# Up projections of a gated MLP by Strassen's seven products, with the down projection dealt between them, in a two-layer encoder kernel on Trainium2

## The chip, the cores and the metric

One core of one Trainium2 chip. The metric is the device time of one execution in microseconds, median of several runs. The kernel before takes 1583.78 us (three runs, 1583.47 to 1584.88).

## The reference, cut to what matters

Two layers of an encoder on 512 tokens of width 1024, all in float32. The attention part of each layer is left out here, since the change does not touch it. The rest of a layer is a gated MLP of width 2816:

```python
hf = rms_norm(x, ffn_norm_g[l])
u = depthwise_conv(hf @ ffn_w_up[l], ffn_conv_w[l], ffn_conv_b[l])   # 512x1024 @ 1024x5632
u_gate, u_val = u[..., :D_FF], u[..., D_FF:]
x = x + (jax.nn.silu(u_gate) * u_val) @ ffn_w_down[l]                # 512x2816 @ 2816x1024
```

## The kernel before

Every matrix product is made of three: each float32 operand is held as a high half, rounded to the type that TensorE multiplies fast (`fp32r`), and a low half, the rest. `mm3` (it calls `mm`, L376) issues high x high, high x low and low x high; low x low is left out. TensorE's moving operand is 512 tokens wide, its stationary operand a 128x128 block of weights or activations.

Weights come as float32 from HBM, in transfers of 128x1024 (`raw<-w`, on SP's queue). `w_split` makes the halves of a piece of 128x512: ScalarE copies it to the high half (`wh<-raw`, L224), and GpSimd, or VectorE where a rule in `pick` says so, subtracts (`wl<-raw,wh`, L231). `wnext` hands TensorE the next piece and has the pieces up to `LA = 3` places ahead split. Lines of the helpers stand for all engines: L224 is every ScalarE activation, L231 every `tensor_tensor`, L235 every `scalar_tensor_tensor`.

The order in which each engine's instructions stand is fixed when the program is built. A class `Clock` counts time by a table of costs per instruction, runs the chains of follow-up work (`chain`, `at`, `need`, `done`) when their inputs should be ready, and so decides where in each engine's queue an instruction stands. At run time each engine works through its queue strictly in that order.

The MLP of a layer works on features x tokens. 22 chunks of 128 features have a gate part and a value part; I call the two a chunk pair. For each part `feat_major` issues 8 x 3 matmuls of 512 columns into one PSUM bank (banks `acc`, `ST` and `AV` in turn), with the weights stationary and the normalised input's halves `HH`, `HL` moving. The normalisation by token (`rbc`) comes after the product. `up_evac` then chains, per part: a VectorE multiplication by `rbc` out of PSUM (`u<-ps_..,rbc`), ScalarE's middle tap of the convolution (`a<-u,prm`), and the two outer taps on VectorE (`a<-u,prm,a`). For the gate follows ScalarE's SiLU; for the value follow the product of the two (`a<-a,a`, VectorE), and its halves (`ah<-a` on ScalarE, `al<-a,ah` on GpSimd). When all 22 chunks are there, the down projection runs: 8 output blocks, each a sum over 22 x 3 matmuls of 512 columns, and a VectorE addition into the residual `XM`. The last output block of the last layer is done in two halves of 256 tokens (`half`), with one bank each (`mi`, `S`).

Of the kernel before, what the change touches and what calls it, by code (L numbers as in the profile page):

```python
# [18 lines left out]
P = 128  # L19
# [13 lines left out]
RAW = 3  # L33
EXTRA = (("q", 2, (2, 5)), ("n", 2, (6, 7)), ("v", 1, (1, 3)))
# [7 lines left out]
LA = 3  # L42
# [7 lines left out]
D_SUM = 2.0  # L50
REST = 0.4
# [33 lines left out]
def _widths():  # L85

    r = [384] * KC + [T] * 8 + [T] * KC + [288] * MID + [T] + [288] * (KC - MID)
    for br in (2, 1, 0):
        late = []
        for k, _ in _order(br):  # L90
            if k in "nv":
                late = WIDTHS[k]
            else:
                r += WIDTHS[k][:1] + late + WIDTHS[k][1:]
                late = []
    return r + [T] * (2 * KC) + [T] * (4 * FC) + [T] * (2 * FC)


def _stream():

    pieces, slots = [], []
    for wd in _widths() * L:
        if len(slots) <= KC or slots[-1] + wd > 1024:
            slots.append(0)
        pieces.append((len(slots) - 1, slots[-1], wd))
        slots[-1] += wd
    return pieces, slots
# [155 lines left out]
def trunk(ctx: ExitStack, tc: tile.TileContext, x, w, prm, gb, cst, out):  # L263
# [57 lines left out]
    pieces, swidth = _stream()  # L321
    soff = np.concatenate([[0], np.cumsum(swidth)]) * P
    st = {"dma": 0, "split": 0, "use": 0}
    raws, halves = {}, {}

    def w_dma():
        i = st["dma"]
        t = slot("raw") if i < KC else rawp.tile([P, 1024], F32, tag="raw", name=f"raw{i}")
        SY.dma_start(t[:, :swidth[i]], w[int(soff[i]):int(soff[i + 1])].rearrange("(p c) -> p c", p=P))
        raws[i] = t  # L330
        st["dma"] += 1

    def w_split():
        j = st["split"]
        sl, off, wd = pieces[j]
        r = raws[sl][:, off:off + wd]
        hi = hlp.tile([P, T], F32R, tag="wh", name=f"wh{j}")
        lo = hlp.tile([P, T], F32R, tag="wl", name=f"wl{j}")
        ck.fin = ck.now
        if j == 0:  # L340
            V.tensor_copy(hi[:, :wd], r)
        else:
            A.activation(hi[:, :wd], r, AF.Copy)
        e = V if j < KC + 3 else pick(W_BIAS, ck.fin + ck.SEM)
        ck.free[e.kind] = max(ck.free.get(e.kind, 0.0), ck.fin + ck.SEM)
        e.tensor_tensor(lo[:, :wd], r, f(hi[:, :wd]), ALU.subtract)
        done("w", j)
        halves[j] = (hi, lo)
        st["split"] += 1
        if j + 1 == len(pieces) or pieces[j + 1][0] > sl:  # L350
            at(ck.fin - ck.now, lambda: w_until(sl + RAW))

# [6 lines left out]
    def w_until(i):  # L359
        while st["dma"] <= min(i, len(swidth) - 1):  # L360
            w_dma()

    def w_ahead(j):
        while st["split"] <= min(j, len(pieces) - 1):
            w_until(pieces[st["split"]][0])
            w_split()

    def wnext():
        j = st["use"]
        w_ahead(j + LA if j > LA else j)  # L370
# [4 lines left out]
    def mm(o, lhsT, rhs, start, stop):  # L375
        PE.matmul(o, lhsT=lhsT, rhs=rhs, start=start, stop=stop)  # L376
        ck.to(ck.now + max(0.107, rhs.shape[-1] / 2370.0))
# [5 lines left out]
    def mm3(o, lh, ll, rh, rl, start, stop):  # L383
        mm(o, lh, rh, start, False)
        mm(o, lh, rl, False, False)
        mm(o, ll, rh, False, stop)
# [14 lines left out]
    MQ, MK = [[cp.tile([P, 4, 4, 96], F32, tag=f"{n}{g}", name=f"{n}{g}") for g in range(2)] for n in ("MQ", "MK")]  # L401
# [132 lines left out]
    def layer(l, sq, xsrc):  # L534
# [6 lines left out]

        gt = slot("gb")
# [913 lines left out]
        def up_evac(c, part, acc, tag):  # L1456
            ci = c + part * FC
            u, a = slot("u"), slot("a")

            def scale():  # L1460
                V.tensor_tensor(u[:, :T], acc, fin["rbc"][:, :T], ALU.mult)
                free(tag)

            steps = [
                ([("rbc", G2)], scale),
# [6 lines left out]
            if part == 0:  # L1472
# [4 lines left out]
                steps.append(gate)  # L1477
            else:
                ah, al = slot("ah", F32R), slot("al", F32R)
                act[c] = (ah, al)  # L1480

                def prod():
                    V.tensor_tensor(a[:, :T], a[:, :T], gated.pop(c)[:, :T], ALU.mult)
                steps += [([("gate", l, c)], prod), *split(ah[:, :T], al[:, :T], a[:, :T], eng=G),
                          lambda: done("act", l, c)]
            chain(*steps)

        n = 0
        norm_begin(G2, sq)
        for c in range(FC):  # L1490
            for part in range(2):
                tag = tags[n % 3]
                n += 1
                acc = ps(tag)
                for i, _ in enumerate(feat_major(acc, G2)):
                    norm_finish(G2, fin, n == 3 and i == 6)
                up_evac(c, part, acc, tag)

        last = l == L - 1
        sq = None if last else slot("sq")  # L1500
        idx, tail = 0, []
        two = [ps(t) for t in ("mi", "S")] if last else None

        def half(n, kc, wh, wl):
            ts = slice(256 * n, 256 * n + 256)
            mm3(two[n][:, :256], wh, wl, act[kc][0][:, ts], act[kc][1][:, ts], kc == 0, kc == FC - 1)
# [6 lines left out]
        for m in range(KC):  # L1513
            tag = tags[m % 3]
            acc = ps(tag)
            for kc in range(FC):
                if idx % 4 == 0:
                    wh, wl = wnext()
                need(("act", l, kc))
                ws = slice((idx % 4) * P, (idx % 4) * P + P)  # L1520
                idx += 1
                if not (last and m == KC - 1):
# [209 lines left out]
```

## Time and profile before

| | |
|---|---|
| median of the runs | 1583.78 us |
| the profiled execution's own time | 1584.02 us |
| its span, first to last instruction | 1581.9 us |
| up projections, layer 0 and layer 1 | about 438 to 688 us, 1219 to 1458 us |
| down projections | about 688 to 808 us, 1458 to 1579 us |
| busy share of the span: PE, DVE, ACT, POOL | 99%, 60%, 50%, 65% |

PE is TensorE, DVE VectorE, ACT ScalarE, POOL GpSimd, SP the engine that issues most transfers. A group's row reads: line, engine, operation, output<-inputs, sizes, count, then busy microseconds and the mean nanoseconds of one, then idle time of the engine just before these instructions and what ended it. An instruction's record overlaps the next one's on the same engine, on PE by much: the pace is read from one start to the next, not from the durations.

### The profile page before, as it was taken

The numbers are of one execution on the slowest core, as the hardware profiler recorded it, in microseconds if no ns is written. First come the engines' busy times: TensorE is split into PE (matmuls) and PEld (weight loads), VectorE is DVE, ScalarE is ACT, GpSimd is POOL, SyncE is SP. The second block draws the span as 40 slices with busy tenths as digits, with TensorE's granted clock in tenths as the row PEclk, the third lists the DMA queues.
The fourth block names the chain that finished last, engine by engine and source line by source line (L and its number), as shares of the span: only waits on it lengthen the run. The fifth ranks groups of instructions, "written<-read, shape, count | busy, mean of one in ns | idle before, by whom it ended". The sixth has DMA issues, their size and how long they took to land.

```text
span 1581.9 us, 20358 instructions
## 1 busy us (share of the span) xinstructions
PE 1567.1 (99%) x7098; PEld 1308.3 (83%) x7098; DVE 946.0 (60%) x1335; ACT 790.7 (50%) x1440; POOL 1023.1 (65%) x901
## 2 busy tenths in 40 slices
PE   9999989999999999999999999899999999999999
PEld 8888878888888888888898888788888888888888
DVE  6867886875267777711046688878652677777000
ACT  5557766763444444432254577676634444444221
POOL 3974876854667666664578658668546676666542
PEclk9999999999999999999999999999999999999999
DMA  6432234314323222233334322343242233223331
GB/s 202 127 115 73 74 91 143 106 62 141 101 91 107 93 94 96 100 115 109 107 111 130 110 74 74 94 138 103 67 147 94 85 109 100 94 93 107 107 126 47
DMA packets 86070, 164.43 MB, mean 104 GB/s; under 512 B 25040, under 2 KB 47056, under 8 KB 85968
## 3 DMA queue, kind: packets, MB, share of 16 engines
q1 hardware_dynamic: 81072, 162.93, 32.4%
q8 instruction: 56, 0.92, 0.2%
q10 hardware_dynamic: 4896, 0.21, 0.2%
q14 instruction: 46, 0.38, 0.1%
HBM read 149.41 MB, written 13.63 MB: 103 GB/s over the span
## 4 chain that ended last, share of the span: by engine, by line
PE 91%; DVE 4%; ACT 2%; DMA 1%; issue 1%; POOL 0%; SPq 0%; ACTq 0%; DVEq 0%
PE ps_acc L376 40%; PE ps_AV L376 22%; PE ps_ST L376 22%; PE ps_S L376 4%; PE ps_mi L376 3%; DVE XM L231 1%; DVE mgl L231 1%; ACT mgh L224 1%; DMA XM<-x 1%; DVE gt L235 0%; DVE sq L231 0%; DMA raw<-w 0%; ACT wh L224 0%; DVE vt L235 0%; ACT ph L224 0%
## 5 line engine op out<-in xcount | busy, mean ns | idle before, releaser
L231 POOL TENSOR_TENSOR wl<-raw,wh 128x512 fp32r<-128x512 f32 (+3 forms) x494 | 668.3, 1364 | 397.5 <-ACT wh L224 377.3
L224 ACT ACTIVATE wh<-raw 128x512 fp32r<-128x512 f32 (+3 forms) x521 | 308.9, 607 | 137.8 <-PE ps_ST L376 46.0
L235 DVE SCALAR_TENSOR_TENSOR a<-u,prm,a 128x511 f32<-128x511 f32 x176 | 243.9, 1388 | 92.6 <-ACT a L224 86.8
L376 PE MATMUL ps_acc<-HH,wh 128*128 128x512 f32 x592 | 231.7, 391 | 3.3 <-DVE vm L231 2.9
L376 PE MATMUL ps_acc<-HH,wl 128*128 128x512 f32 x592 | 231.2, 391 | 0.0
L376 PE MATMUL ps_acc<-HL,wh 128*128 128x512 f32 x592 | 231.1, 390 | 0.0
L376 PEld LDWEIGHTS ps_acc<-HH,wh 128*128 128x128 f32 x592 | 111.4, 188 | 26.4 <-issue 4.4
L376 PEld LDWEIGHTS ps_acc<-HH,wl 128*128 128x128 f32 x592 | 111.2, 188 | 23.8
L376 PEld LDWEIGHTS ps_acc<-HL,wh 128*128 128x128 f32 x592 | 111.3, 188 | 22.8
L376 PE MATMUL ps_AV<-HH,wh 128*128 128x512 f32 x288 | 112.3, 390 | 0.0
L376 PE MATMUL ps_AV<-HH,wl 128*128 128x512 f32 x288 | 112.2, 390 | 0.0
L376 PE MATMUL ps_AV<-HL,wh 128*128 128x512 f32 x288 | 112.2, 390 | 0.0
L231 POOL TENSOR_TENSOR al<-a,ah 128x512 fp32r<-128x512 f32 x44 | 58.0, 1319 | 83.5 <-ACT ah L224 79.4
L239 DVE TENSOR_REDUCE nm<-ps_S 128x1 fp32r<-128x512 f32 x128 | 87.7, 685 | 36.0 <-PE ps_S L376 34.6
L376 PE MATMUL ps_ST<-HH,wh 128*128 128x512 f32 x240 | 93.6, 390 | 0.0
L376 PE MATMUL ps_ST<-HL,wh 128*128 128x512 f32 x240 | 93.4, 389 | 0.0
L376 PE MATMUL ps_ST<-HH,wl 128*128 128x512 f32 x240 | 93.4, 389 | 0.0
L224 ACT ACTIVATE ah<-a 128x512 fp32r<-128x512 f32 x44 | 27.8, 632 | 128.8 <-DVE a L231 128.8
L224 ACT ACTIVATE a<-u,prm 128x512 f32<-128x512 f32 x88 | 70.9, 808 | 23.4 <-DVE u L231 23.2
L224 ACT ACTIVATE a<-a 128x512 f32<-128x512 f32 x44 | 27.6, 632 | 104.7 <-DVE a L235 104.7
L224 ACT ACTIVATE HH<-XM,prm 128x512 fp32r<-128x512 f32 x32 | 23.1, 722 | 103.5 <-DVE XM L231 53.7
L224 ACT ACTIVATE ps_ST<-ps_ST 128x512 f32<-128x512 f32 x86 | 49.8, 582 | 32.9 <-PE ps_ST L376 31.2
(374 smaller groups left out, 3734.9 us busy)
## 6 DMA issues: line engine op xcount, KB each, us to landing
raw<-w SPq DMA_DIRECT2D x230, 512.0 KB, 3.4
raw<-w SPq DMA_DIRECT2D x14, 384.0 KB, 3.1
XM<-x SPq DMA_DIRECT2D x16, 256.0 KB, 3.7
dtq<-tr SPq DMA_DIRECT2D x16, 192.0 KB, 1.9
dtk<-tr SPq DMA_DIRECT2D x16, 192.0 KB, 1.9
tf<-dtq SPq DMA_DIRECT2D x48, 64.0 KB, 2.0
tf<-dtk SPq DMA_DIRECT2D x48, 64.0 KB, 2.1
xsp<-XM SPq DMA_DIRECT2D x8, 256.0 KB, 2.0
```

What stands on the lines that cost most here:

```text
L224: return self.eng.activation(out, in_, func, **k)
L231: return self.eng.tensor_tensor(out, *a)
L235: return self.eng.scalar_tensor_tensor(out, *a)
L239: return self.eng.tensor_reduce(out, in_, *a, **k)
L376: PE.matmul(o, lhsT=lhsT, rhs=rhs, start=start, stop=stop)
```

## The change

Of the 22 chunk pairs of a layer, 5 (group 0) are computed as before. For the other 17, the 2x2 block matrix of (gate and value part) x (even and odd 128-feature blocks of the input) meets the 2x2 matrix of (even and odd input blocks) x (first and second 256 tokens), and `product` multiplies them with Strassen's seven products (Winograd's form) in place of eight. One product is 4 x 3 matmuls of 256 columns.

- **Token side**, once per layer (`build_forms`): the normalised input is formed explicitly (`hn`, 8 VectorE instructions of 512 columns), GpSimd makes its sums (`tt`, 16 of 256 columns), and the 7 x 4 forms are split into halves (`tf`, 28 ScalarE copies and 28 VectorE subtractions of 256 columns).
- **Weight side**, per pair (`w_form`): four pieces of 128x512 are loaded, each by a transfer of its own. Three of the seven forms are plain pieces; the four others are sums that VectorE makes (`raw<-raw,raw`, `s<-raw,raw` ...), and their low halves are made on VectorE too.
- **Low halves by transfer** (`by_transfer`): for the three plain forms, and for all weights of group 0, ScalarE writes the high half and its negative, and a transfer issued by GpSimd adds the raw weights to the latter. GpSimd's subtraction goes.
- **After the products**, per pair: four ScalarE copies of 256 columns out of PSUM (`sx`), and four VectorE additions of 256 columns (`u<-ps_..,sx`) in place of the two multiplications by `rbc`. The chain from the convolution on is kept.
- **Down projection** in five groups of chunks (`SIZES`): the blocks of one group are dealt between the products of the next (`_ffn`), with bank `mi` or `S`; each group ends in its own addition to the residual, so 40 in place of 8 per layer. The matmuls are as many as before. 8 blocks of group 3 and all of group 4 come after the last pair.
- The weights are made `LAF = 5` places ahead near such products.

```diff
-LA = 3
+LA, LAF = 3, 5
+SIZES = (5, 4, 4, 4, 5)
+KEEP = 2
+FORMS = ("11", "12", "1", "22", "2", "4", "3")
+SPOTS = ("22", "2", "4", "3")
...
+    def by_transfer(hi, lo, r):
+        A.activation(hi, r, AF.Copy)
+        A.activation(lo, f(hi), AF.Copy, scale=-1.0)
+        ck.free["Pool"] = max(ck.free.get("Pool", 0.0), ck.fin + ck.SEM)
+        ck.took("Pool", D_ISSUE)
+        nc.gpsimd.dma_start(f(lo), r, accum_op=ALU.add)
+        ck.fin += D_ADD
...
+        dst, x, y, op, keys, gone = {
+            "1": (a21, a21, a22, ALU.add, [], None),
+            "2": (s2, a21, a11, ALU.subtract, [("sum", pi, "1")], 0),
+            "4": (a12, a12, s2, ALU.subtract, [("sum", pi, "2")], None),
+            "3": (s2, a22, s2, ALU.subtract, [("sum", pi, "4"), ("form", pi, "2")], 3)}[form]
+        def total():
+            V.tensor_tensor(dst, x, y, op)
...
+        def low():
+            V.tensor_tensor(lo[:, :T], dst, f(hi[:, :T]), ALU.subtract)
...
+        chain((keys, total), lambda: A.activation(hi[:, :T], dst, AF.Copy), low, after=0.0)
...
     def wnext():
         j = st["use"]
-        w_ahead(j + LA if j > LA else j)
+        n = LAF if any(units[min(i, len(units) - 1)][0] not in "pu" for i in (j, j + LAF)) else LA
+        w_ahead(j + n if j > LA else j)
...
+        def product(c, name):
...
+            for q in range(4):
+                need(("tf", l, name, q))
+                ws, d = slice(q * P, q * P + P), forms[name, q]
+                mm3(o, wh[:, ws], wl[:, ws], d[:, 0:256], d[:, 256:512], q == 0 and name in ("11", "12", "1", "22"),
+                    q == 3, name not in ("12", "22"))
...
+            if name == "11":
+                aside(sa[:, lo], "s1")
+            elif name == "12":
+                chain(([("s1", l, c)], add(u[:, lo], sa[:, lo], "ST")))
+            elif name == "1":
+                aside(sb[:, lo], "s5")
+            elif name == "22":
+                aside(sb[:, hi], "s4", "ST")
+            elif name == "2":
+                aside(sa[:, hi], "s2")
+            elif name == "4":
+                chain(([("s2", l, c)], add(u[:, hi], sa[:, hi], "AV")), *convolve(c, 0, u))
             else:
+                chain(([("s4", l, c)], add(v[:, hi], sb[:, lo])), add(v[:, lo], sb[:, hi], "acc"), *convolve(c, 1, v))
...
+        for kind, *tok in _ffn():
+            {"u": plain, "f": product, "d": down}[kind](*tok)
```

The order of the instructions outside the two MLP parts is the same in both kernels, on every engine. Three places within them:

TensorE's queue, in the up projection of layer 0, before: one part of a pair, 24 such rows to a bank.

```order
L376 MATMUL ps_acc_5266<-HH,wh_5223 128x512
L376 MATMUL ps_acc_5266<-HL,wh_5223 128x512
L376 MATMUL ps_acc_5266<-HH,wl_5224 128x512
```

The same queue in the changed kernel, at the end of product "22" of a pair of group 2 and the start of the dealt block behind it (`tf` a token form, `fh`, `fl` the halves of a weight form made by transfer).

```order
L507 MATMUL ps_ST_6284<-tf_4735,fh_6173 128x256 x2
L507 MATMUL ps_ST_6284<-tf_4735,fl_6174 128x256
L507 MATMUL ps_ST_6284<-tf_4742,fh_6173 128x256 x2
L507 MATMUL ps_ST_6284<-tf_4742,fl_6174 128x256
L507 MATMUL ps_mi_6310<-HH,wh_6187 128x512
L507 MATMUL ps_mi_6310<-HL,wh_6187 128x512
L507 MATMUL ps_mi_6310<-HH,wl_6188 128x512
```

Up to eight matmuls of 512 columns on one input block pair have become seven times three of 256 columns, and the down projection's blocks stand between the products.

VectorE's queue, layer 0, before: one chunk pair from the gate's multiplication to the product of the two parts.

```order
L231 TENSOR_TENSOR u_5704<-ps_acc_5662,rbc_4676 128x512
L235 SCALAR_TENSOR_TENSOR a_5705<-u_5704,prm_92,a_5705 128x511 x2
L231 TENSOR_TENSOR u_5746<-ps_ST_5706,rbc_4676 128x512
L235 SCALAR_TENSOR_TENSOR a_5747<-u_5746,prm_92,a_5747 128x511 x2
L231 TENSOR_TENSOR a_5747<-a_5747,a_5705 128x512
```

The same queue in the changed kernel, the first twelve rows of one pair's round in group 2 (`raw` and `s` are weights and their sums, `sx` the copies of other products, `XM` the residual). The round ends with the rest of these: a low half, a tap, the addition of the next pair's first half, the product of the parts, a sum and two low halves.

```order
L289 TENSOR_TENSOR raw_6104<-raw_6104,raw_6118 128x512
L289 TENSOR_TENSOR XM<-ps_mi_6310,XM 128x512
L289 TENSOR_TENSOR wl_6349<-raw_6104,wh_6348 128x512
L289 TENSOR_TENSOR u_6216<-ps_AV_6263,sx_6218 128x256
L293 SCALAR_TENSOR_TENSOR a_6366<-u_6216,prm_91,a_6366 128x511 x2
L289 TENSOR_TENSOR u_6217<-ps_acc_6220,sx_6219 128x256 x2
L289 TENSOR_TENSOR s_963_6417<-raw_6104,raw_6039 128x512
L289 TENSOR_TENSOR XM<-ps_S_6372,XM 128x512
L293 SCALAR_TENSOR_TENSOR a_6399<-u_6217,prm_91,a_6399 128x511
L289 TENSOR_TENSOR wl_6416<-s_963_6417,wh_6415 128x512
L289 TENSOR_TENSOR raw_6064<-raw_6064,s_963_6417 128x512
L293 SCALAR_TENSOR_TENSOR a_6399<-u_6217,prm_91,a_6399 128x511
```

The seven instructions of a pair have become 19: eight for weight forms and two for the residual have come in among them, and two multiplications have become four half-width additions.

GpSimd's queue, layer 0, before: some two chunk pairs' worth.

```order
L231 TENSOR_TENSOR wl_5004<-raw_4887,wh_5003 128x512
L231 TENSOR_TENSOR wl_5026<-raw_4931,wh_5025 128x512
L231 TENSOR_TENSOR wl_5048<-raw_4931,wh_5047 128x512
L231 TENSOR_TENSOR wl_5070<-raw_4975,wh_5069 128x512
L231 TENSOR_TENSOR al_5045<-a_5043,ah_5044 128x512
```

The same queue in the changed kernel, one pair of group 2 (here the activation's low half is written to `HL`, whose old content is used up).

```order
L289 TENSOR_TENSOR wl_6382<-raw_6120,wh_6381 128x512
L289 TENSOR_TENSOR wl_6459<-raw_6120,wh_6458 128x512
L289 TENSOR_TENSOR HL<-a_6399,HH 128x512
L420 DMA fl_6500<-raw_6232 128x512
L420 DMA fl_6518<-raw_6258 128x512
L420 DMA fl_6562<-raw_6312 128x512
```

Five subtractions per pair (four for its up weights, one for its activation) have become three (two for the dealt down weights) and three issues of adding transfers.

More of the change, by code (lines that the diff above doesn't have):

```diff
@@ L539, in col @@
             return pr[:, i:i + 1]
+        MQ, MK = [[mp.tile([P, 4, 4, 96], F32, tag="m", name=f"{n}{l}{g}") for g in range(2)] for n in ("MQ", "MK")]
         gt = slot("gb")
@@ L1489, in layer, with prod @@
[L1489 to L1497, printed above, removed]
+                return steps + [gate]
+            ah, al = act[c] = keep_act(c)
+            def prod():
+                V.tensor_tensor(a[:, :T], a[:, :T], gated.pop(c)[:, :T], ALU.mult)
```

375 lines of the change are left out of this document (286 added, 89 removed).

## The prediction

> **What bounds the kernel now.** I read the page first, then the chain of work that ended last, then the two MLP parts by stretches and groups.
>
> ```profile
> span 1581.9 us, 20358 instructions
> ...
> PE 1567.1 (99%) x7098; PEld 1308.3 (83%) x7098; DVE 946.0 (60%) x1335; ACT 790.7 (50%) x1440; POOL 1023.1 (65%) x901
> ...
> PEclk9999999999999999999999999999999999999999
> ```
>
> TensorE is busy 99% of the span at the full granted clock. "Busy" can hide a slow pace, so I look at pieces of the chain in order of time: one part of a pair (24 matmuls of 512 columns) and one output block of the down projection (66).
>
> ```profile
> 1229.63 5.45 PE ps_AV L376 x24
> ...
> 1458.12 14.96 PE ps_acc L376 x66
> ```
>
> 5.44 to 5.45 us for 24 and 14.96 for 66 are both 0.2267 us a matmul. A pair costs 48 x 0.2267 = 10.88 us. And TensorE hardly waits for anyone; the longest rows of its waits, over the whole program:
>
> ```profile
> PE ps_acc L376 <- DVE vm L231: 2.9, 2, 1.5
> PE ps_ST L376 <- ACT vt L224: 2.5, 2, 1.3
> PE ps_AV L376 <- DVE ph L247: 1.7, 2, 0.9
> ```
>
> So the time goes with TensorE's own work, until another engine can't keep up. The other engines during layer 0's up projection:
>
> ```profile
> core 0: us, PE busy (x) PEld busy (x) DVE busy (x) ACT busy (x) POOL busy (x), PEclk, DMA share, GB/s
> 448.50:688.00 239.50, 239.50 (x1058) 198.35 (x1057) 168.05 (x155) 107.84 (x177) 162.28 (x111) 1.00 0.30 99
> ```
>
> DVE and POOL are busy some 70% there already. That is the reserve which the change draws on.
>
> **Term 1: TensorE's work.** The pace of 256 columns is in the trace: the last output block of the last layer is done in two halves, 132 matmuls.
>
> ```profile
> 1562.68 0.28 PE L376 MATMUL ps_mi<-ah,wh 128*128 128x256 f32 x1
> ...
> 1578.39 0.28 PE L376 MATMUL ps_S<-ah,wl 128*128 128x256 f32 x1
> ...
> 1562.68:1578.52 15.84, 15.84 (x133) 15.78 (x131) 1.12 (x2) 0.00 (x0) 0.67 (x1) 1.00 0.05 18
> ```
>
> 131 steps in 15.71 us are 0.120 us each, a little over half of 0.2267, though weight loads (PEld) fill 15.78 of the 15.84 us. A pair by seven products is 7 x 12 = 84 such matmuls, 10.08 us: 0.80 less than 10.88. For 17 pairs in two layers that is 34 x 0.80 = **27.2 us** off. One eighth of the work would be 46; the fixed part of each matmul takes the rest. Group 0 and the down projection's matmuls are as many as before, and the order outside the MLP is the same, so nothing else changes on TensorE unless it waits.
>
> **Term 2: can VectorE keep up?** What it costs per instruction, and what it loses beside GpSimd, from the groups of layer 0's up projection:
>
> ```profile
> L231 POOL TENSOR_TENSOR wl<-raw,wh 128x512 fp32r<-128x512 f32 x89 | 135.2, 1534 | 32.3 <-ACT wh L224 32.1
> L235 DVE SCALAR_TENSOR_TENSOR a<-u,prm,a 128x511 f32<-128x511 f32 x88 | 122.1, 1390 | 46.9 <-ACT a L224 43.5 <-POOL wl L231 1.9
> L224 ACT ACTIVATE wh<-raw 128x512 fp32r<-128x512 f32 x88 | 54.0, 616 | 0.7 <-issue 0.7
> L224 ACT ACTIVATE a<-u,prm 128x512 f32<-128x512 f32 x44 | 35.5, 808 | 11.4 <-DVE u L231 11.3
> L231 POOL TENSOR_TENSOR al<-a,ah 128x512 fp32r<-128x512 f32 x22 | 29.0, 1319 | 41.7 <-ACT ah L224 39.7 <-PE ps_acc L376 2.0
> L231 DVE TENSOR_TENSOR a<-a,a 128x512 f32<-128x512 f32 x22 | 16.2, 737 | 1.3 <-ACT a L224 0.6
> ```
>
> and the shortest, median and longest of them over both layers, with the two halves at the end:
>
> ```profile
> L235 DVE SCALAR_TENSOR_TENSOR a<-u,prm,a x176: 739/1658/1885, 450.1 to 1461.1; 128x511 f32<-128x511 f32 x176
> L231 DVE TENSOR_TENSOR a<-a,a x44: 691/693/1667, 457.6 to 1462.8; 128x512 f32<-128x512 f32 x44
> L231 DVE TENSOR_TENSOR u<-ps_ST,rbc x30: 676/692/692, 448.6 to 1458.2; 128x512 f32<-128x512 f32 x30
> L231 DVE TENSOR_TENSOR XM<-ps_mi,XM x1: 425/425/425, 1577.6 to 1577.6; 128x256 f32<-128x256 f32 x1
> ```
>
> A tap of the convolution takes 0.74 us at its shortest and 1.66 in the median; with one operand in PSUM it is 0.69 and never more. The long ones are those that meet a subtraction on GpSimd:
>
> ```profile
> 570.48 2.98 POOL L231 TENSOR_TENSOR wl<-raw,wh 128x512 fp32r<-128x512 f32 x2
> 570.74 3.27 DVE L235 SCALAR_TENSOR_TENSOR a<-u,prm,a 128x511 f32<-128x511 f32 x2 [0.95 <-ACT a L224]
> ```
>
> Two taps beside two subtractions: 3.27 for 1.48, so 0.9 us lost to each. Over the stretch the taps lose 88 x (1.390 - 0.739) = 57 us to its 111 GpSimd subtractions: **0.52 us per GpSimd subtraction** on average, since not each meets a tap. I call this price p; it is the number on which the result hangs.
>
> A pair of groups 2 and 3 in the changed kernel gives VectorE: 8 weight sums and low halves and one product of 512 columns, taken at 0.69 (same operation and operands as `a<-a,a`), 6.21; 4 taps at 0.74, 2.96; 4 additions of 256 columns out of PSUM at 0.425, 1.70; 2 residuals at 0.69, 1.38. Together 12.25 us. To it come waits within the fixed order. Before, 43.5 us of waiting for ScalarE in 44 parts are 1.0 us a part: a tap stands straight behind the addition that ScalarE must first work on. Now one of the two parts has other work in between, but the low half of form "3" stands straight behind its sum and waits for a copy of 0.62 with two others queued ahead of it: 1.0 again, 2.0 per pair, 14.25 us. GpSimd does 3 subtractions, costing 3p. TensorE needs 10.08 + 8 blocks x 3 x 0.2267 = 15.52 us for the same pair.
>
> By groups, VectorE against TensorE per pair, at p = 0, 0.52 and 1.0:
> - Groups 2 and 3 (8 pairs): 14.25, 15.8, 17.25 against 15.52. Late by 0, 0.3, 1.7.
> - Group 1 (4 pairs, 10 dealt blocks, 3.5 subtractions): 14.25, 16.1, 17.75 against 16.88. Late by 0, minus 0.8, 0.9.
> - Group 4 (5 pairs, 4.8 blocks, 1.2 residuals, 2.2 subtractions): 13.7, 14.8, 15.9 against 13.34. Late by 0.4, 1.5, 2.6. Here the pairs stand closest, and it is where I expect the waits.
> - Group 0, once `rbc` is there, has 43 us. VectorE gets 10 multiplications, 8 `hn`, about 20 taps, 4 products, 28 half-width subtractions and 4 weight steps: 6.9 + 5.9 + 14.8 + 2.8 + 11.9 + 2.8 = 45 us by records; these overlap by some 0.08 each where they stand close (about 74 of them), so 39. GpSimd's 16 half-width sums and 4 subtractions add about 12p: 39, 45.5, 51. Late by 0, 2, 8; group 1 gives the 2 back.
>
> A pair has 9 weight places, so five places ahead are 8.6 us. A form needs 0.69 + 0.62 + 0.69 with hand-overs, 2.2, and some 2.1 behind others in the queue. **4.3 us** of lateness per layer cost nothing. Beyond it TensorE waits in full, for weights. Behind the last pair stand 8 + 4 blocks, 8.2 us, before the last activation is needed, against a chain of some 6.5; there VectorE has no next pair's 5.5 us of forms to make and can catch up.
>
> Lateness per layer at p = 0.52: 8 x 0.3 + 5 x 1.5 = 9.9, minus 4.3, so 5.6 of waiting; **11 us** in two layers. At p = 0 none; at p = 1.0, 8 + 3.6 + 13.6 + 13 = 38, minus 4.3, 67 us in two layers. I take 0.52, the mean of the nearest rows: VectorE's queue will be denser than before, which raises the share of subtractions that meet something, but 6 of its 19 instructions read PSUM, and some of what is lost falls into the 2.0 us in which it waits anyway.
>
> A rule of the Trainium skill speaks against the change: in "SBUF — State Buffer", section "Who interferes with whom", a VectorE instruction with two SBUF inputs and a GpSimd instruction that reads SBUF exclude each other for the whole instruction, whoever comes first. The trace agrees in kind: 0.74 against 1.66, and never over 0.69 with PSUM. By that rule alone every subtraction that meets VectorE's queue could cost up to its whole 1.29 us; the measured 0.52 is what I go by. The page infers that issuing transfers from GpSimd does not meet such instructions; no run here shows it.
>
> **Term 3: edits that I cost at nothing.** ScalarE gets 14 activations of 0.62, two of 0.81 and four of at most 0.62 per pair, 12.8 us at most of 15.52 (records overlap by a tenth), so it is the next bound, and covered only while VectorE serves it. The adding transfers have no row. Their flight is at least 2.0 us (a transfer within the chip) and at most about 5.5 (the slowest of SP's), their issue on GpSimd 0.33 (SP's) to 1.3 us (as long as a subtraction):
>
> ```profile
> dtq<-tr SPq DMA_DIRECT2D x16, 192.0 KB, 1.9
> ...
> C<-cst SPq DMA_DIRECT2D x1, 552.0 KB, 5.5
> ```
>
> ```profile
> L1540 SPq DMA_DIRECT2D xsp<-XM x8: 326/326/327, 688.1 to 792.9; - x8
> ```
>
> With two copies of 0.62 that is 3.6 to 8.0 us, within the 8.6 of five places and the 8.2 of three places of 2.72 in group 0. I take the middle, no wait; at the upper end, with anything queued ahead, 1 us per pair, 34. Queued behind such an issue on GpSimd are the subtractions for the dealt weights; 3 x 1.3 + 3 x 1.0 us leave GpSimd free for half of the pair. The loads, 0.75 MB more per pair moved within the chip, meet transfer engines at a share of 0.30. The bank of a product is read by ScalarE while three other products (4.3 us) run, against 0.6 for the copy.
>
> **Sum.** From the profiled execution's 1584.0 (0.2 us off the median): 1584.0 - 27.2 + 11 = **1568 us**.
>
> **Rivals.**
> - *VectorE and GpSimd cost each other more* (slower). The place is group 4 and the second half of group 2 on. From 0.52 to 1.0 the lateness grows by 28 us per layer, 58 per us of p. The gain is gone when it reaches 13.6 + 4.3 = 17.9 per layer, at p = 0.66. For it: the 0.9 lost per meeting in the rows, and a denser queue. Against: the mean of 0.52. At p = 0.8 it is 26 - 4.3 = 22 per layer: 1584 - 27 + 44 = 1601 us.
> - *Nothing waits*: the losses fall into gaps. 1584.0 - 27.2 = 1557 us. For it: 14.25 under 15.52; against: group 4 is late even at p = 0.
> - *The adding transfers land late* (their price above): 1568 + 34 = 1602.
> - *It doesn't do what it says*: if the 256-column matmuls came at over 10.88 / 84 = 0.1295 us, nothing would be saved, some 1595. PEld at 15.78 of 15.84 speaks for it; that the same three matmuls on the same kinds of operands made 0.120 speaks against.
>
> **How the numbers follow.** The forecast 0.46; nothing waits 0.14; the first rival 0.25; late transfers 0.06; no saving 0.03; the remaining 0.06 for ending between, where p is near 0.66. A measurement of this kernel can tell 0.2% from no change. Faster by over 0.2%: 0.60; within: 0.06; slower: 0.34. The forecast's own range is 1558 to 1579; the range with the rivals reaches from 1555, just under "nothing waits", to 1603, which leaves out the upper end of the first rival and of the transfers.
>
> **What would show it.** Term 1: 12 matmuls of a product in 1.44 us, and TensorE's starts 0.120 apart. Term 2: rows of TensorE waiting for VectorE's or GpSimd's weight halves (`wl`, `fl`) or for the last activation, mostly in group 4; VectorE's `wl<-s` and `wl<-raw` between 0.69 and 1.7 with a mean about 1.0. If those are near 0.7, "nothing waits" is right; if most are near 1.7 and waits begin in group 2, the first rival is. Waits for `fl` or for group 0's `wl` by a transfer point to the third. The forecast fails most easily on p and on the 4.3 us of lead.

## The result, and the profile after

The changed kernel takes **1612.87 us** (median of 4 runs, 1611.15 to 1614.14) against 1583.72 for the kernel before on the same chip (1583.47 to 1584.88): ratio 1.0182, 95% interval 1.0164 to 1.0200. The forecast was 1568. The profiled execution took 1611.84 us. Its page, of the kernel after, with the totals and the chain that ended last:

```profile
span 1610.1 us, 23869 instructions
...
PE 1556.5 (97%) x8271; PEld 1341.0 (83%) x8271; DVE 1179.9 (73%) x1811; ACT 988.1 (61%) x1876; POOL 923.1 (57%) x899
...
PE 65%; DVE 17%; ACT 8%; issue 5%; DMA 3%; POOL 2%; SPq 0%; ACTq 0%; DVEq 0%; POOLq 0%
```

The time grew although TensorE's busy time fell by 10.6 us. VectorE and ScalarE now hold 25% of the chain, against 6% in the kernel before. TensorE's timeline, of the kernel after, in the MLP of both layers (start, duration, and in brackets the wait ahead and what ended it):

```profile
480.06 0.80 PE L507 MATMUL ps_ST<-HH,wl 128*128 128x512 f32 x1 [3.73 <-DMA wl<-raw]
...
725.15 0.50 PE L507 MATMUL ps_acc<-tf,wh 128*128 128x256 f32 x2 [1.61 <-ACT sx L282]
...
769.05 0.50 PE L507 MATMUL ps_acc<-tf,wh 128*128 128x256 f32 x2 [1.11 <-ACT sx L282]
...
1299.67 0.80 PE L507 MATMUL ps_acc<-HH,wl 128*128 128x512 f32 x1 [4.96 <-DMA wl<-raw]
```

These are the longest wait of each layer, in group 0, and the two longest of layer 0's last group. All waits over 2 us stand in group 0 (468 to 500 and 1267 to 1302), and their operand is a plain weight half `wl`, not a form. The same timeline at the borders: where layer 0's MLP starts, its first product, the first matmul behind the MLP; where layer 1's MLP and its first product start, and two products in a row:

```profile
432.96 0.39 PE L507 MATMUL ps_acc<-HH,wh 128*128 128x512 f32 x1
...
502.87 0.40 PE L507 MATMUL ps_acc<-tf,fh 128*128 128x256 f32 x2
...
805.90 0.33 PE L507 MATMUL ps_acc<-wh,HH 128*128 128x384 f32 x1
...
1232.31 0.39 PE L507 MATMUL ps_acc<-HH,wh 128*128 128x512 f32 x1
...
1306.66 0.40 PE L507 MATMUL ps_acc<-tf,fh 128*128 128x256 f32 x2
...
1557.49 0.40 PE L507 MATMUL ps_acc<-tf,fh 128*128 128x256 f32 x2
1558.91 0.28 PE L507 MATMUL ps_ST<-tf,fh 128*128 128x256 f32 x1
```

The ten plain parts of group 0 need 54.5 us of matmuls (240 x 0.2267, and 0.1 for the sum of squares), so the first product should start at 487.5 and 1286.8. It starts 15.4 and 19.8 us later: **35 us** of loss before the first pair by seven products. The whole MLP of layer 0 takes 805.90 - 432.96 = 372.9 us, 13.7 more than the 359.3 of the kernel before, whose borders are:

```profile
432.65 0.39 PE L376 MATMUL ps_acc<-HH,wh 128*128 128x512 f32 x1
...
791.93 0.33 PE L376 MATMUL ps_acc<-wh,HH 128*128 128x384 f32 x1
```

In it the pairs give back 16.0 us: a product of 12 matmuls lasts 1.42 us, seven 9.94, 0.94 less than 10.88, in 17 pairs. So 29.7 us are lost in layer 0: 15.4 in group 0, and 14.3 behind it. What the engines did in group 0 of layer 0 (433 to 503 us), VectorE's four costliest groups and two of GpSimd's (the sums have three groups, 16 in all, 1.06 to 1.14 us each):

```profile
L293 DVE SCALAR_TENSOR_TENSOR a<-u,prm,a 128x511 f32<-128x511 f32 x17 | 15.4, 913 | 1.7 <-ACT a L282 1.7
L293 DVE SCALAR_TENSOR_TENSOR hn<-XM,prm,rbc 128x512 f32<-128x512 f32 x8 | 14.1, 1760 | 0.0
L289 DVE TENSOR_TENSOR tf<-hn,tf 128x256 fp32r<-128x256 f32 x12 | 8.3, 712 | 0.0
L289 DVE TENSOR_TENSOR tf<-tt,tf 128x256 fp32r<-128x256 f32 x15 | 8.0, 550 | 2.6 <-ACT tf L282 2.6
```

```profile
L289 POOL TENSOR_TENSOR tt<-hn,tt 128x256 f32<-128x256 f32 x8 | 8.2, 1064 | 0.0
L289 POOL TENSOR_TENSOR al<-a,ah 128x512 fp32r<-128x512 f32 x4 | 5.7, 1425 | 2.7 <-ACT ah L282 2.7
```

The shortest, median and longest of the two kinds of instruction that VectorE makes for the forms:

```profile
L289 DVE TENSOR_TENSOR tf<-hn,tf x24: 409/412/4965, 454.4 to 1282.6; 128x256 fp32r<-128x256 f32 x24
L293 DVE SCALAR_TENSOR_TENSOR hn<-XM,prm,rbc x16: 739/743/7059, 449.0 to 1264.3; 128x512 f32<-128x512 f32 x16
```

Against 0.743, 0.412 and 0.739 us the four groups have 8.1 + 3.6 + 2.1 + 3.0 = 16.8 us too much, beside 16 sums and 4 subtractions on GpSimd: 0.84 us each. One instruction carries much of it. VectorE and GpSimd from 464 to 472 us:

```profile
464.95 7.06 DVE L293 SCALAR_TENSOR_TENSOR hn<-XM,prm,rbc 128x512 f32<-128x512 f32 x1
471.93 0.74 DVE L293 SCALAR_TENSOR_TENSOR a<-u,prm,a 128x511 f32<-128x511 f32 x1
```

```profile
464.83 1.05 POOL L289 TENSOR_TENSOR tt<-hn 128x256 f32<-128x256 f32 x1
465.60 1.64 POOL L289 TENSOR_TENSOR tt<-hn,tt 128x256 f32<-128x256 f32 x2
466.98 1.50 POOL L289 TENSOR_TENSOR al<-a,ah 128x512 fp32r<-128x512 f32 x1
468.19 1.12 POOL L420 DMA_DIRECT2D wl<-raw  x1
468.81 1.28 POOL L289 TENSOR_TENSOR tt<-hn 128x256 f32<-128x256 f32 x1
469.50 1.27 POOL L289 TENSOR_TENSOR tt<-hn,tt 128x256 f32<-128x256 f32 x1
470.19 1.26 POOL L289 TENSOR_TENSOR tt<-hn,hn 128x256 f32<-128x256 f32 x1
```

GpSimd runs eight instructions without a gap, from 464.83 to 471.45. VectorE's multiplication starts 0.12 us after the first of them and ends 0.56 us behind the last, 7.06 us for 0.74: it isn't held by one instruction of GpSimd, but by the whole run, and the issue of a transfer in the middle did not let it in. An issue alone held nothing there: one at 464.22 lasts 0.89 us, and a tap beside it, at 464.29, takes its usual 0.74. Nor does every run hold to its end. A subtraction on VectorE that was held from 477.13 on ended 0.29 us behind a sum (its end is at 479.49), while the next issue ran and two sums were still to come; in layer 1 the same instruction was held through the whole run, for 4.96 us.

```profile
477.13 2.65 DVE L289 TENSOR_TENSOR tf<-hn,tf 128x256 fp32r<-128x256 f32 x1
```

```profile
479.25 1.08 POOL L420 DMA_DIRECT2D wl<-raw  x1
```

From the hold of 7.06 us the longest wait of layer 0 follows step by step. ScalarE's next instruction, and a later issue on GpSimd:

```profile
473.31 0.81 ACT L282 ACTIVATE a<-u,prm 128x512 f32<-128x512 f32 x1 [6.87 <-DVE u L289]
```

```profile
476.63 0.88 POOL L420 DMA_DIRECT2D wl<-raw  x1 [5.18 <-ACT wl L282]
```

ScalarE waits 6.87 us for VectorE. Behind that activation, in its fixed order, stand the copies for the next weight halves. GpSimd is idle for 5.18 us until such a copy is there, issues the transfer at 476.63, and TensorE starts with its result at 480.06. So the wait that names a transfer comes from VectorE, and this transfer did not queue behind the sums on GpSimd. A shorter wait did come in part from that queue: the issue at 468.19 stands 2 us behind its copy, in the middle of the run, and TensorE waited 1.16 us for it, to 471.75.

### The profile page after: what moved, and what is told of

Same layout as the page of the kernel before. It is cut to its first block, busy times and chain, and to the rows that moved or that the text cites. A ratio compares the mean times of both kernels' runs of the same rounds, so it can differ in the third digit from the quotient of the medians.

```text
span 1610.1 us, 23869 instructions
## 1 busy us (share of the span) xinstructions
PE 1556.5 (97%) x8271; PEld 1341.0 (83%) x8271; DVE 1179.9 (73%) x1811; ACT 988.1 (61%) x1876; POOL 923.1 (57%) x899
## 3 DMA queue, kind: packets, MB, share of 16 engines
q8 instruction: 65, 1.06, 0.3%
## 4 chain that ended last, share of the span: by engine, by line
PE 65%; DVE 17%; ACT 8%; issue 5%; DMA 3%; POOL 2%; SPq 0%; ACTq 0%; DVEq 0%; POOLq 0%
PE ps_acc L507 30%; PE ps_AV L507 13%; PE ps_ST L507 11%; PE ps_S L507 6%; PE ps_mi L507 6%; DVE a L293 5%; DVE hn L293 2%; DVE XM L289 2%; ACT wh L282 2%; DVE wl L289 2%; DVE u L289 1%; DMA fl<-raw 1%; DVE tf L289 1%; DVE s L289 1%; ACT a L282 1%
## 5 line engine op out<-in xcount | busy, mean ns | idle before, releaser
L289 POOL TENSOR_TENSOR wl<-raw,wh 128x512 fp32r<-128x512 f32 (+3 forms) x318 | 412.0, 1302 | 363.6 <-ACT wh L282 336.2
L282 ACT ACTIVATE wh<-raw 128x512 fp32r<-128x512 f32 (+2 forms) x453 | 267.7, 605 | 91.6 <-DVE raw L289 50.4
L507 PE MATMUL ps_acc<-HH,wl 128*128 128x512 f32 x416 | 164.2, 395 | 11.1 <-DMA wl<-raw 11.1
L420 POOL DMA_DIRECT2D fl<-raw x102 | 89.6, 878 | 119.9 <-ACT sx L282 39.8
L289 DVE TENSOR_TENSOR wl<-raw,wh 128x512 fp32r<-128x512 f32 (+2 forms) x96 | 90.0, 938 | 37.0 <-ACT wh L282 36.1
L507 PE MATMUL ps_acc<-tf,wh 128*128 128x256 f32 x544 | 100.9, 284 | 5.9 <-ACT sx L282 5.8
L507 PE MATMUL ps_AV<-tf,wh 128*128 128x256 f32 x544 | 100.3, 282 | 1.0 <-ACT sx L282 1.0
L507 PE MATMUL ps_ST<-tf,fh 128*128 128x256 f32 x544 | 100.1, 282 | 0.0
L507 PEld LDWEIGHTS ps_acc<-tf,wh 128*128 128x128 f32 x544 | 87.4, 189 | 14.5 <-ACT sx L282 9.7
L507 PEld LDWEIGHTS ps_AV<-tf,wh 128*128 128x128 f32 x544 | 86.1, 190 | 4.6 <-ACT sx L282 1.9
L507 PEld LDWEIGHTS ps_ST<-tf,fh 128*128 128x128 f32 x544 | 83.9, 190 | 0.0
```

The source lines that it names most:

```text
L282: return self.eng.activation(out, in_, func, **k)
L289: return self.eng.tensor_tensor(out, *a)
L420: nc.gpsimd.dma_start(f(lo), r, accum_op=ALU.add)
L507: PE.matmul(o, lhsT=lhsT, rhs=rhs, start=start, stop=stop, skip_group_check=again)
```

## The experiments

**The theories.** Theory 1: in group 0 the 16 token sums per layer on GpSimd come in runs that hold VectorE off; the activations' work and the forms stand behind it, ScalarE waits for VectorE in its fixed order, and group 0's weight halves, prepared only three places ahead, come late. Theory 2: the adding transfers that now make these weight halves are too slow for three places. Theory 3: VectorE has too much to do in group 0, whoever makes the sums. All ratios are to the kernel before on the same chip.

**e1: the sums on VectorE.**

```
-                return [([("hn", l, 2 * q), ("hn", l, 2 * q + 1)], lambda: G.tensor_tensor(t[0][:, lo], ...
+                return [([("hn", l, 2 * q), ("hn", l, 2 * q + 1)], lambda: V.tensor_tensor(t[0][:, lo], ...
...
(the other three sums of each q alike)
```

> The 16 half-width token sums per layer go from GpSimd to VectorE. Theory 1 (runs of these sums on GpSimd hold VectorE off in group 0, ScalarE and the weights stand behind it): VectorE gets 16 x 0.35 = 5.6 us of work per layer and is spared the 14 us by which its records there exceed their shortest; group 0's delay falls from 15 to 20 us per layer to about 3 to 5, the total to some 1586 us (1580 to 1593). Theory 2 (the adding transfers of group 0's weights land too late, whatever VectorE does): 1613, within 4. Theory 3 (VectorE simply has too much to do in group 0): 5 to 6 us per layer worse, 1620 to 1626.

Measured 1598.2 us, ratio 1.0089 [1.0074, 1.0104]: 14.7 us of the loss (0.93% of 1583.7) are gone, though VectorE has 32 instructions more. Theory 2 had expected no change and theory 3 a loss. But theory 1 had expected nearly twice as much, and at most 1593 us. The multiplications, and the sums that VectorE now makes:

```profile
L293 DVE SCALAR_TENSOR_TENSOR hn<-XM,prm,rbc x16: 739/747/749, 451.8 to 1261.9; 128x512 f32<-128x512 f32 x16
L289 DVE TENSOR_TENSOR tt<-hn,tt x16: 411/414/424, 459.1 to 1274.2; 128x256 f32<-128x256 f32 x16
```

No `hn` lasts over 0.75 us, and a sum takes 0.41 where GpSimd takes 1.06. Group 0 loses 3.1 and 1.6 us in the two layers instead of 15.4 and 19.8. What is left comes right behind: TensorE waits for activations of group 0 in the first dealt blocks.

```profile
505.60 0.55 PE L507 MATMUL ps_mi<-ah,wh 128*128 128x512 f32 x1 [2.02 <-ACT ah L282]
509.90 0.80 PE L507 MATMUL ps_mi<-al,wh 128*128 128x512 f32 x1 [3.75 <-POOL al L289]
```

VectorE comes out of group 0 with a backlog, and where the weights no longer wait for it, the down projection does.

**e2: group 0's weights by subtraction, and e3: both.**

```
-        if kind == "u":
+        if False:
             by_transfer(hi[:, :wd], lo[:, :wd], r)
```

> Only the 20 weight halves per layer of group 0 lose their adding transfers: one copy on ScalarE and a subtraction on GpSimd or VectorE, as in the kernel before. Theory 1: the sums hold VectorE as before, and the subtractions queue among them on GpSimd: group 0 keeps 10 us or more of delay per layer, 1605 to 1625 us. Theory 2: group 0's delay goes almost whole, 1578 to 1588. Theory 3: ScalarE is spared 20 x 0.63 us per layer, VectorE gets a few subtractions: 1605 to 1620.

> Both edits: token sums on VectorE, group 0's weight halves by subtraction. Theory 1: no run of sums is left, but 20 subtractions of 1.3 us on GpSimd each cost VectorE about 0.5 in a dense queue, 10 us per layer: between the first experiment and the kernel after, 1585 to 1603 us. Theory 2: as the second experiment, 1578 to 1590. Theory 3: VectorE has most to do of all, 1620 or more.

Measured 1615.25 us, ratio 1.0194 [1.0179, 1.0209], and 1611.92 us, ratio 1.0168 [1.0151, 1.0185]. Theory 2 had expected 1578 to 1590 of both. Without any adding transfer in group 0, e2 still loses 12.1 us there in each layer, so the loss as a whole doesn't come from the transfers. That they have no part in it can't be read from e2 alone, since subtracting has a price of its own: with the sums on VectorE it costs 12.5 us more than transferring (1.0168 against 1.0089). But e1 kept every transfer, and group 0's loss fell from 35 us to 5. One part of theory 2 does show in the kernel after: the last two transfers of group 0 in layer 1 take 7.0 and 7.6 us from issue to landing, against 3.8 in the median, in a stretch (1295 to 1300) in which the transfer engines are busy all the time, and the wait of 4.96 us is for the first of them. At 3.8 us it would have been some 3 us shorter. e3 came out 9 us above the top of theory 1's interval, about as much as e1, on which it is built, had missed its own forecast (12).

**e4: no sums at all, and e9: sums that nobody reads.**

```
-                t = tt.pop(q)
-                chain(([("tt", l, q)], lambda: None), *halve("1", q, t[0][:, 0:256]), *halve("22", q, t[1][:, 256:512]),
-                      *halve("2", q, t[0][:, 256:512]), *halve("3", q, t[1][:, 0:256]), after=0.0)
+                chain(*halve("1", q, a[:, 0:256]), *halve("22", q, b[:, 256:512]),
+                      *halve("2", q, a[:, 256:512]), *halve("3", q, b[:, 0:256]), after=0.0)
...
-                      lambda: (chain(*sums(q), after=0.0), parts(q)), ...
+                      lambda: parts(q), ...
```

(e9 keeps the line of the last two as it was.)

> The 16 token sums per layer are left out: forms 1, 2, 3 and 22 are cut from the normalized halves themselves, so the output isn't the reference's; all matmuls, weight forms and copies stay. Theory 1: group 0's delay goes almost whole, 1575 to 1584 us, and no multiplication for the normalized activations lasts over 2 us. Theory 2: 1613, within 4. Theory 3: VectorE's own work is unchanged, 1605 to 1613.

> As the fourth experiment (forms 1, 2, 3 and 22 cut from the normalized halves, so the output isn't the reference's), but GpSimd still makes the 16 sums per layer, and nothing reads them. Theory 1a (the sums cost by holding VectorE off while they run): near the kernel after, 1600 to 1613 us, with a VectorE instruction of several us in group 0 again. Theory 1b (they cost because VectorE and ScalarE, in their fixed order, wait for their results): as the fourth experiment, 1583 to 1590.

Measured 1586.06 us without the sums, ratio 1.0014 [1.0004, 1.0023], and 1609.0 us with the unread sums, ratio 1.0155 [1.0138, 1.0171]. The two differ only in 32 GpSimd instructions whose results nothing waits for, and in some neighbouring instructions of VectorE and ScalarE that have changed places; the 32 cost 22 us, 0.7 us each. They fall in group 0: it loses 17.7 and 17.4 us in e9, 7.9 and 5.8 in e4. Waiting for the sums' results can account for about the 4.3 us between e9 and the kernel after, whose intervals overlap. VectorE and GpSimd in the run with unread sums:

```profile
477.85 4.27 DVE L293 SCALAR_TENSOR_TENSOR a<-u,prm,a 128x511 f32<-128x511 f32 x1
```

```profile
477.93 1.04 POOL L289 TENSOR_TENSOR tt<-hn,hn 128x256 f32<-128x256 f32 x1
478.63 1.57 POOL L289 TENSOR_TENSOR al<-a,ah 128x512 fp32r<-128x512 f32 x1
479.86 1.70 POOL L289 TENSOR_TENSOR tt<-hn,tt 128x256 f32<-128x256 f32 x2
```

A tap ends at 482.12, 0.56 us behind the end of GpSimd's run at 481.56. That is theory 1 in its form 1a. But e4 came out 2 us above theory 1's interval, and it still loses 7.9 us in group 0 of layer 0 (first product at 495.69, start at 433.28). A stretch of it:

```profile
460.00:470.00 10.00, 8.57 (x38) 6.72 (x38) 10.00 (x20) 9.90 (x23) 4.42 (x4) 1.00 0.75 145
```

The columns are TensorE, weight loads, VectorE, ScalarE and GpSimd, each busy time and count, then granted clock, DMA share and GB/s. VectorE is busy 10.0 of 10 us, and ScalarE 9.9: here both are at their end even without the sums, as theory 3 has it. But e1, where VectorE has more to do, loses less in group 0 than e4 and more behind it, so the amount of VectorE's work doesn't set group 0's loss alone; how the order of the forms' work shares the loss between the two places was not tested.

**e5 and e6: more plain pairs in front, fewer pairs at the end.** Sums on VectorE as in e1, and

```
-SIZES = (5, 4, 4, 4, 5)
+SIZES = (7, 4, 4, 4, 3)
```

or (6, 4, 4, 4, 4).

> Token sums on VectorE as in the first experiment, and groups of 7, 4, 4, 4 and 3 chunks: seven plain pairs while the forms are built, and three pairs in the last group, each with 8 dealt blocks instead of 4.8. Theory 1 (what is lost is VectorE's backlog out of group 0 and the too short pairs of the last group): the first experiment lost some 11 us per layer in group 0 and just behind it, where TensorE waited for al, and 5 in the last group; both go almost whole, and two pairs fewer by seven products cost 2 x 2 x 0.8 = 3.2: 1598 - 26 + 3 = 1575 (1568 to 1583), below the kernel before. Rival (the pairs themselves lose, wherever they stand): the waits move into the next group, 1592 to 1603.

> The same with groups of 6, 4, 4, 4 and 4. Theory 1: half of the relief, most of group 0's and a third of the last group's: 1598 - 16 + 1.6 = 1584 (1577 to 1590). Rival: 1595 to 1602.

Measured **1575.12 us**, ratio 0.9943 [0.9928, 0.9957], faster than both kernels, and 1576.71 us, ratio 0.9954 [0.9939, 0.9969]. The seventh plain pair brings almost nothing over the sixth, and six relieve more than the half that I expected (1577 at best). Of TensorE's waits in the run of seven (total, times, longest) these two are the largest in the MLP:

```profile
PE ps_acc L507 <- DMA wl<-raw: 4.8, 3, 2.6
...
PE ps_acc L507 <- DMA fl<-raw: 2.2, 4, 0.8
```

No wait for `al`, `ah` or `sx` is left among the rows. The forecast of 1575 was met, but not in all its parts: group 0 itself still loses 5.4 and 4.2 us, no less than in e1, and what went are the waits behind it and in the last group.

**e10: seven plain pairs with the sums left on GpSimd.** Only the SIZES of e5.

> Groups of 7, 4, 4, 4 and 3 as in the fifth experiment, with the token sums left on GpSimd. Theory 1: the hold falls in the first third of the forms, where TensorE waits for group 0's weights at once, however many parts follow: 8 to 15 us above the fifth experiment, 1583 to 1590. Rival (only the room behind the forms matters): 1575 to 1578.

Measured 1603.42 us, ratio 1.0116 [1.0101, 1.0131]: 27 us above e5, where theory 1 had said 8 to 15 and the rival none. The first product comes 18.8 and 19.1 us late, against 5.4 and 4.2 in e5, and that is the whole difference: the hold costs as soon as it occurs, and room behind it doesn't bring it back. Between the kernel after and e1 group 0 gained as much, 30 us, but the time only 14.7: there the rest was paid again behind group 0, where e1's waits for `ah` and `al` in the first dealt blocks add up to 5.8 and 5.4 us, and in e5 these are gone.

**e7: the pairs' low halves by subtraction.** In the kernel after, `by_transfer` for the forms "11", "12" and "22" becomes

```
-            by_transfer(hi[:, :T], lo[:, :T], {"11": a11, "12": a12, "22": a22}[form])
+            r = {"11": a11, "12": a12, "22": a22}[form]
+            A.activation(hi[:, :T], r, AF.Copy)
+            e = pick(W_BIAS, ck.fin + ck.SEM)
...
+            e.tensor_tensor(lo[:, :T], r, f(hi[:, :T]), ALU.subtract)
```

> From the kernel after: the three low halves per pair that come by adding transfers (102 in all) come by a subtraction on GpSimd again. GpSimd has 3 x (1.3 - 0.87) = 1.3 us more per pair, ScalarE 3 x 0.63 = 1.9 less. Theory A (each GpSimd subtraction costs VectorE 0.52 us, as the prediction took from the kernel before): 1.6 us per pair more for VectorE, which has no gap left in groups 2 and 3: up to 34 x 1.6 = 53, less the slack, 1640 to 1665 us. Theory B (in the pairs few meet, as the taps' mean of 0.98 in place of 1.39 suggests; loss 0.2 each): 0.6 per pair fits into the gaps, and with the transfers' lateness gone 1605 to 1620.

Measured 1638.27 us, ratio 1.0342 [1.0327, 1.0357]: 25 us above the kernel after, 0.25 us for each of 102 subtractions. It lies between the two theories' intervals, next to A's: gaps take some of it, but far from all.

**e8 and e11: the down projection in groups alone.** All pairs plain:

```
-            for f in FORMS:
-                toks.append(("f", c, f))
...
+            for k in range(2):
+                toks.append(("u", c, k))
+                toks += now[len(now) * k // 2:len(now) * (k + 1) // 2]
```

with weights by subtraction and no forms; e11 also keeps the middle groups' activations in slots instead of `HH` and `HL`.

> Only the down projection in five groups is kept: all 22 pairs are plain, 48 matmuls of 512 columns, with weight halves by subtraction as before, no forms and no adding transfers; the dealt blocks stand behind the parts of each pair. Theory 1 (the loss is all in the seven products' supply): as the kernel before, 1580 to 1588 us. Rival (the grouped down projection costs by itself, by its 32 more residual additions per layer and its interleaving): 1590 to 1605.

> The down projection in five groups alone, as in the eighth experiment, now with the activations of the middle groups in tiles of their own, so that no pair's operands are written over: all 22 pairs plain, weight halves by subtraction. Theory 1: grouping costs next to nothing, 1582 to 1590 us, and the whole loss of the kernel after belongs to the seven products' supply. Rival: grouping costs by itself, 1592 to 1605; then a part of the loss in the pairs is its.

The first was a failed experiment: its activations overwrite `HH` and `HL`, which plain pairs still read, so its output isn't the reference's, and its 1626.16 us, ratio 1.0266 [1.0248, 1.0283], contain waits for these tiles; nothing follows from it. The second measured 1584.71 us, ratio 1.0002 [0.9993, 1.0011]. The down projection in five groups costs nothing that can be measured, so the loss belongs to the seven products and what feeds them.

**e12: a longer lead.** e5 with LA = 4 and, to make room, NSLOT = 45.

> The fifth experiment with weights prepared four places ahead in place of three wherever no form is near (one more pair of weight tiles, two slots fewer). If the rest that TensorE waits for group 0's weights (8.6 us for adding transfers in the fifth experiment's trace) is a matter of lead: 1567 to 1572. If ScalarE and VectorE, which are busy 9.9 and 10.0 us of 10 there, are the limit: 1573 to 1577.

Measured 1590.09 us, ratio 1.0036 [1.0025, 1.0048], 15 us worse than e5 and outside of both expectations. In the stretch of 480 to 490 us, in which e5 waits 2.6 us for `wl`, TensorE is busy 10.00 of 10 us with 46 matmuls; but elsewhere new waits stand, the largest in the pairs:

```profile
PE ps_ST L507 <- DMA fl<-raw: 12.8, 10, 2.7
```

In that stretch, then, a lead of one more place was enough; whether the longer lead or the two slots fewer made the new waits stays open, since both were changed at once.

## Why the prediction was wrong

**Term 1 was right, and a little low.** Products take 1.42 us instead of 1.44: 34 x 0.94 = 32 us off, where 27.2 were forecast.

**Term 2 failed at group 0.** This is the step that made the forecast wrong. The prediction put group 0 late by "0, 2, 8" for p = 0, 0.52 and 1.0, of which "group 1 gives the 2 back". It was 15.4 and 19.8 us late, and gave nothing back. Three things were wrong in that step.
- The price. The prediction had 12p, 6.2 us, for GpSimd's 16 sums and 4 subtractions; 16.8 us were lost beside them, 0.84 each. In the prediction's own line 39 + 16.8 against 43 would be 12.8 us late, most of the 15.4. A sum of half the width was taken at half the price, but it lasts 1.06 us where a subtraction of full width lasts 1.30. And the old mean of 0.52 came mostly from single subtractions with waits for ScalarE between them, while the sums stand in runs, and a VectorE instruction that meets a run mostly pays for the run. The Trainium skill says in "SBUF — State Buffer", section "Who interferes with whom", that a VectorE instruction with two SBUF inputs and a GpSimd instruction that reads SBUF exclude each other, for the whole instruction; the trace goes further, with 7.06 us through a run of eight.
- ScalarE. It was summed for a pair, where it has room, and not for group 0, where 28 copies of form halves and 20 second copies of weights come on top; e4 shows it busy 9.9 of 10 us. In the kernel after this didn't bind yet: there ScalarE is busy 4.6, 6.3 and 5.4 of 10 us from 460 to 490, since it waits for VectorE.
- The lead. I set 4.3 us of slack per layer against the sum of all lateness. That is the lead of five places in the pairs. Group 0 has three places, lateness there falls in a stretch of 30 us, and what TensorE lost at 468 to 500 no later slack could return. With four places, in e12, group 0 loses 1.5 and 1.9 us where e5 loses 5.4 and 4.2.

A part is the clock. Behind the longest of these waits the granted clock was lower; of the kernel after, layer 0:

```profile
480.00:490.00 10.00, 9.94 (x35) 8.02 (x36) 8.46 (x11) 5.38 (x11) 6.03 (x8) 0.78 0.47 107
```

35 matmuls instead of the 46 of a full stretch, at 0.78, with hardly a wait: 2.4 us. In layer 1 two such stretches, 1275 to 1285 and 1295 to 1305, stand at 0.66; 18 matmuls there come about 0.43 us apart instead of 0.2267, 3.9 us in all. So some 6 of the 35 us are the clock. The rows of waits have 11.1 and 13.8 of them.

**Term 2 in the pairs was nearer.** Behind group 0, 14.3 us were lost in layer 0 and, by the span, about 25 in both, where 11 were forecast. The rows of waits behind group 0 add up to 7.7 us in layer 0; the other 6.6 stand in no such row, and their cause stays open. In group 3 nothing waited. Its stretch, of the kernel after, with TensorE busy 60.00 of 60 us (a pair and its 8 dealt blocks take 15.53), and VectorE's groups in it:

```profile
640.00:700.00 60.00, 60.00 (x416) 55.91 (x415) 50.25 (x73) 40.28 (x77) 27.56 (x24) 1.00 0.61 144
```

```profile
L293 DVE SCALAR_TENSOR_TENSOR a<-u,prm,a 128x511 f32<-128x511 f32 x16 | 15.5, 972 | 3.7 <-ACT a L282 3.5
L289 DVE TENSOR_TENSOR raw<-raw,s 128x512 f32<-128x512 f32 x4 | 7.1, 1777 | 0.0
L289 DVE TENSOR_TENSOR wl<-s,wh 128x512 fp32r<-128x512 f32 x8 | 5.5, 686 | 5.3 <-ACT wh L282 5.3
```

VectorE is busy 13.0 us per pair, not the 14.25 and 1.56 for GpSimd that I had added. The price isn't what was too high: taps and one weight sum lose 3.7 + 4.4 = 8.1 us beside 12 subtractions, 0.67 each. Its own 19 instructions cost about 11 instead of 12.25, since records overlap, and 10 of the 60 us are gaps in which the waits for ScalarE lie. So `wl<-s` stands at 0.69, the mark that I had set for "nothing waits".

**Group 4: right place, another wait.** In layer 0 TensorE's two long waits there, 1.61 and 1.11 us, are for `sx`, ScalarE's copy of a product's bank, and one of 0.3 for a weight form. I had costed the copy at nothing, because three other products run meanwhile. ScalarE's timeline, of the kernel after, ahead of the wait of 1.11:

```profile
766.37 0.63 ACT L282 ACTIVATE wh<-s 128x512 fp32r<-128x512 f32 x1 [2.33 <-DVE s L289]
...
768.63 0.37 ACT L282 ACTIVATE sx<-ps_acc 128x256 f32<-128x256 f32 x1
```

The copy stands in ScalarE's order behind a weight copy that waits 2.33 us for VectorE's sum `s`, with three instructions between. With fewer dealt blocks to a pair TensorE comes back for it too soon; in e5, with 8 blocks, it no longer does.

**Term 3 held, but for the end of group 0.** Of the kernel after, the adding transfers of group 0 (median from issue to landing in us), and those of the tile `fl`: their issue on GpSimd in ns and their landing:

```profile
wl<-raw POOLq DMA_DIRECT2D x40, 256.0 KB, 3.8
```

```profile
L420 POOL DMA_DIRECT2D fl<-raw x102: 859/874/1055, 494.6 to 1556.6; - x102
...
DMA to landing us min/median/max: 3.3/5.2/7.9
```

The medians of 3.8 and 5.2 us lie within the bounds of 2.0 to 5.5, only the longest are above: 7.9 in the pairs, and 7.6 at the end of group 0, where it cost the 3 us named under e2; the issue of 0.87 lies within 0.33 to 1.3. The waits for `fl` add up to 2.8 us in layer 0. And the transfers pay: e7 takes them away from the pairs and loses 25 us; e3 takes them from group 0 and loses 12 against e1. With the sums on GpSimd (e2 against the kernel after) the same step in group 0 measures nothing.

**The rivals.** The one on the other side had the right cause, VectorE and GpSimd costing each other more, but the wrong place: it was to begin in groups 2 and 4, and its point of decision, p = 0.66, was worked out for pairs. p was 0.67 there, and the pairs of group 3 lost nothing by it. "Adding transfers late" gave 1602, not far from the measured time, by another mechanism: TensorE's waits in group 0 name these transfers, but the longest of layer 0 was issued late because VectorE was held, and only some 3 us of the longest of layer 1 are the transfer's own. And the sum: 1584.0 - 32 + 35 + 25 = 1612, in which the 25 is what the span leaves, so that it closes by construction.

## What to carry to other kernels

Price what one engine costs another by how densely the two will stand, not by a mean from a stretch with gaps: here a run of back-to-back GpSimd instructions held a VectorE instruction with two SBUF operands mostly until the run's end, so work that GpSimd seems to take off VectorE can be cheaper on VectorE itself (0.41 us against 1.06, and no hold). Slack counts only at the place and time where the lateness falls; sum every engine for the transition stretch as well as for the steady one. And before a schedule is given up, move its edges: groups of 7, 4, 4, 4 and 3 with the sums on VectorE turned 1.8% slower into 0.6% faster.

## What the hardware showed that I had not expected

- A VectorE instruction of 0.74 us lasted 7.06 us beside eight consecutive GpSimd instructions, one of them a transfer's issue; in e9 one that started 0.08 us ahead of the first sum of a run, beside a transfer's issue, was held through the run, 4.27 us. In both it ended 0.56 us behind the run's end. The one at 477.13 got in earlier, during an issue.
- Matmuls of 256 columns come 0.118 us apart in a product of 12 (1.42 us), a little closer than the 0.120 of the last output block.
- Behind each of the three waits of 3.6 to 5.0 us in group 0, nine or ten matmuls of 512 columns come about 0.43 us apart instead of 0.2267, and the stretch of 10 us stands at a granted clock of 0.78 or 0.66. Behind the shorter waits they come at their usual pace.
- An adding transfer of 256 KB within the chip takes 5.2 us in the median and up to 7.9, of which GpSimd is held 0.87 by the issue.
